# Down projection by seven block products: operand sums from the up stage, residual summed in DRAM

## The chip, the core and the metric

One core of a Trainium2 chip runs the whole kernel. Its engines work side by side, each on its own queue in order: TensorE (PE, with PEld for its weight loads), VectorE (DVE), ScalarE (ACT), GpSimd (POOL) and SyncE (SP). DMA transfers are issued here from SP's and POOL's queues. The metric is the device time of one execution in microseconds (us). Three executions of the kernel before took 2852.30, 2852.07 and 2847.18 us, median 2852.07.

## The reference

One layer of a hybrid decoder on 512 prompt tokens and 8 x 4 sample tokens, all in float32, model width 2048, feed-forward width 5504. Attention (two groups of heads) comes first; the part that matters here is the feed-forward block with a causal convolution of width 3 over the tokens, and the gate behind it:

```
def conv_ffn(xn, prefix, w_up, conv_w, conv_b, w_down):
    L = xn.shape[1]
    a, u = jnp.split(xn @ w_up, 2, axis=-1)
    a_all = jnp.concatenate([prefix.astype(a.dtype), a], axis=1)
    c = a_all[:, 0:L] * conv_w[0] + a_all[:, 1:L + 1] * conv_w[1] + a_all[:, 2:L + 2] * conv_w[2] + conv_b
    h = jax.nn.gelu(c) * u
    return h @ w_down, a_all[:, -(CONV_W - 1):]
...
        f, conv_new = conv_ffn(rmsnorm(h, ffn_norm_g[i]), conv_s[i], ffn_w_up[i], ffn_conv_w[i],
                               ffn_conv_b[i], ffn_w_down[i])
        h = h + f
        h = h + jax.nn.sigmoid(h @ ple_w_gate[i] + ple_b_gate[i]) * (p[i] @ ple_w_proj[i])
    y = rmsnorm(h, final_norm_g)
```

## The kernel before

**Layout.** Features lie on the 128 partitions, tokens are columns: 544 of them, as two halves of 272 (256 prompt and 16 sample tokens each). The width 2048 is 16 tiles of 128 rows, the feed-forward width 5504 is 43 tiles, which I call hidden tiles.

**Products.** A float32 product is made from two parts of each number, a high part (a cast, on ACT) and a low part (the difference, on DVE), and three matmuls: high by high, high by low, low by high (`product`, line 176; `multiply`, line 1146). So weights are loaded raw by SP, cast to wh by ACT (line 166, or 1138 in up) and subtracted to wl by DVE (167 or 1139), and the moving operands are split in the same way (886 and 887). One matmul is 128x128 weights by 128x272 columns.

**Up.** For each hidden tile, `up` computes both the gate half a and the linear half u of the tile for both halves of the tokens. That is a product of a 2x2 block matrix of weights by a 2x2 block matrix of operands (blocks of 8 of the 16 width tiles), and it is made by seven products in place of eight, from sums of blocks: the operand sums a11, s1, s2, a12, s3, s4, a22 lie in SBUF for the whole stage, and the weight sums are made per tile by DVE on the raw tiles (lines 1171, 1177, 1187, 1194). Each product is 8 x 3 = 24 matmuls, 168 a tile, into three PSUM banks X, Y, Z. The sums over the results, the normalisation, the convolution and the gelu follow on DVE, ACT and POOL (lines 1196 to 1217); the hidden tile uu goes to DRAM (hd, line 1218, by SP). POOL copies the last rows of the convolution into one tile cvo for all hidden tiles (lines 1205 and 1206), stored once at the end.

**Down.** The residual, 16 tiles resid, comes back from DRAM (rd, line 1254, by POOL). Then two phases of 22 and 21 hidden tiles: POOL loads each hidden tile (hr, line 1262), ACT and DVE split it into hh and hl, which stay in SBUF for the phase; for each of the 16 output tiles, 6 matmuls per hidden tile (three, for two halves of the columns) into one PSUM tile, which DVE adds to resid (line 1271). 

**Gate and end.** resid is split into h2, the gate product (16 x 96 matmuls) and the per-layer embedding follow, then the final normalisation.

**What sets the order.** A scheduler puts each engine's instructions in a fixed order when the kernel is built; on the chip each engine's queue runs in that order and waits by semaphores. Buffers come from pools with a number of turns (`bufs`): an instruction that writes the next turn waits until the readers of the old one are done. In this program a DMA of SP or POOL is issued only when the eighth one before it on the same queue has landed.

## Time and profile before

| what | value |
|---|---|
| times of three runs | 2852.30, 2852.07, 2847.18 us |
| the profiled execution's own time | 2849.02 us |
| its span | 2847.2 us |
| mean granted clock of TensorE | 0.978 |
| PE busy in the span | 2747.2 us, 96% |
| DVE, ACT, POOL busy | 1549.0, 1026.9, 381.0 us |
| up, steady part | about 1330 to 2042 us of the span |
| down | 2067.6 to 2622.2 us |
| gate | 2622.2 to 2820.2 us |

The profiled execution is 3.0 us below the median of the three. Busy times of engines overlap. A busy PE includes matmuls at the lower clock, so the granted clock stands beside it wherever a stretch is read. An instruction's mean is over all its occurrences in the run.

### The profile page before, as it was taken

To read this page: it belongs to the slowest core of one execution; us is meant where nothing else is said; L and a number is where in the kernel's file an instruction comes from. 1 tells how busy PE (TensorE), PEld (TensorE's weight loads), DVE (VectorE), ACT (ScalarE), POOL (GpSimd) and SP (SyncE) were. 2 spreads that over 40 slices of the span, in tenths; PEclk is the share of its full clock that TensorE was granted. 3 is DMA by queue.
4 is the path that set the end of the run, shared out by engine and by line. 5 is a ranking of instruction groups with operands and counts; after the bars stand their busy time and mean duration, and the time that the engine had idled before them with its cause. 6 is when DMAs were issued, how large, how long until landed. Compare 5 with 4: busy or idle time off the path is not lost.

```text
span 2847.2 us, 50928 instructions
## 1 busy us (share of the span) xinstructions
PE 2747.2 (96%) x21730; PEld 2681.2 (94%) x21730; DVE 1549.0 (54%) x2245; ACT 1026.9 (36%) x1621; POOL 381.0 (13%) x492
## 2 busy tenths in 40 slices
PE   8999999999999999899999999999959999999996
PEld 7989999999999789899999999999959999999996
DVE  5034433322256668878888888888742224223344
ACT  4034323221135455544544445445431113112331
POOL 6610101101201300111111111111130001000001
PEclk9999999999999999999999999999979999999998
DMA  6422222332524814333333333433273225223321
GB/s 228 149 72 77 93 91 84 109 106 94 196 75 175 294 51 143 116 112 112 106 129 102 114 121 101 126 110 107 77 265 94 85 86 160 87 89 102 113 91 68
DMA packets 103699, 335.36 MB, mean 118 GB/s; under 512 B 13105, under 2 KB 17857, under 8 KB 100401
## 3 DMA queue, kind: packets, MB, share of 16 engines
q1 hardware_dynamic: 86432, 271.76, 29.0%
q0 software_dynamic: 17040, 60.36, 6.4%
q8 instruction: 170, 2.79, 0.4%
q14 instruction: 57, 0.46, 0.0%
HBM read 289.87 MB, written 42.19 MB: 117 GB/s over the span
## 4 chain that ended last, share of the span: by engine, by line
PE 82%; issue 10%; DMA 3%; DVE 3%; POOL 1%; ACT 1%; SPq 0%; DVEq 0%; POOLq 0%; ACTq 0%
PE mp L176 35%; PE X L1146 18%; PE Y L1146 9%; PE mq L176 6%; PE Z L1146 4%; DMA hr<-hd 2%; PE sp L357 2%; PE sp L963 1%; PE sp L923 1%; PE sp L593 1%; POOL rows L336 1%; PE sp L944 1%; PE so L585 1%; DMA raw<-in_w_out 0%; DVE resid L1325 0%
## 5 line engine op out<-in xcount | busy, mean ns | idle before, releaser
L167 DVE TENSOR_TENSOR wl<-raw,wh 128x1024 fp32r<-128x1024 f32 (+3 forms) x271 | 307.9, 1138 | 538.1 <-ACT wh L166 514.0
L166 ACT CAST wh<-raw 128x1024 fp32r<-128x1024 f32 (+3 forms) x271 | 263.9, 976 | 846.5 <-PE mp L176 629.2
L1138 ACT CAST wh<-raw 128x1024 fp32r<-128x1024 f32 x301 | 312.3, 1051 | 369.7 <-PE X L1146 153.1
L1139 DVE TENSOR_TENSOR wl<-raw,wh 128x1024 fp32r<-128x1024 f32 x301 | 363.9, 1220 | 63.5 <-ACT wh L1138 61.5
L176 PE MATMUL mp<-xl,wh 128*128 128x272 f32 x1408 | 303.3, 294 | 0.0
L176 PE MATMUL mp<-xh,wl 128*128 128x272 f32 x1408 | 301.3, 294 | 0.0
L176 PE MATMUL mp<-xh,wh 128*128 128x272 f32 x1408 | 300.0, 293 | 0.0
L176 PEld LDWEIGHTS mp<-xh,wl 128*128 128x128 f32 x1408 | 225.8, 191 | 5.7 <-issue 5.2
L176 PEld LDWEIGHTS mp<-xl,wh 128*128 128x128 f32 x1408 | 225.8, 191 | 4.3 <-issue 3.7
L176 PEld LDWEIGHTS mp<-xh,wh 128*128 128x128 f32 x1408 | 225.0, 191 | 4.0 <-issue 2.7
L176 PE MATMUL mp<-hh,wh 128*128 128x272 f32 x946 | 198.8, 292 | 28.8 <-ACT hh L886 28.8
L176 PE MATMUL mp<-hl,wh 128*128 128x272 f32 x946 | 196.9, 290 | 0.7 <-DVE hl L887 0.7
L176 PE MATMUL mp<-hh,wl 128*128 128x272 f32 x946 | 196.8, 290 | 0.0
L176 PEld LDWEIGHTS mp<-hh,wh 128*128 128x128 f32 x946 | 149.2, 190 | 30.3 <-ACT hh L886 30.3
L176 PEld LDWEIGHTS mp<-hl,wh 128*128 128x128 f32 x946 | 150.1, 190 | 2.0 <-DVE hl L887 1.9
L1205 POOL COPY cvo<-ae 128x2 f32<-128x2 f32 x43 | 51.6, 1200 | 738.8 <-DVE ae L1202 738.8
L176 PEld LDWEIGHTS mp<-hh,wl 128*128 128x128 f32 x946 | 149.4, 190 | 0.1
L1146 PE MATMUL Y<-s,wh 128*128 128x272 f32 x688 | 133.3, 289 | 4.7 <-ACT uu L1174 4.7
L1146 PE MATMUL X<-a,wh 128*128 128x272 f32 x688 | 131.3, 288 | 0.0
L1146 PEld LDWEIGHTS Y<-s,wh 128*128 128x128 f32 x688 | 109.0, 190 | 5.0 <-ACT uu L1174 5.0
L1146 PEld LDWEIGHTS X<-a,wh 128*128 128x128 f32 x688 | 108.4, 189 | 0.2 <-DVE uu L1189 0.2
L1146 PE MATMUL Z<-a12h,wh 128*128 128x272 f32 x344 | 99.9, 291 | 0.4 <-ACT wh L1138 0.4
(463 smaller groups left out, 6932.6 us busy)
## 6 DMA issues: line engine op xcount, KB each, us to landing
raw<-in_w_up SPq DMA_DIRECT2D x172, 512.0 KB, 4.6
raw<-in_w_in SPq DMA_DIRECT2D x89, 512.0 KB, 3.5
raw<-in_w_dn SPq DMA_DIRECT2D x64, 512.0 KB, 3.6
raw<-in_w_gate SPq DMA_DIRECT2D x32, 512.0 KB, 3.7
raw<-in_w_out SPq DMA_DIRECT2D x24, 512.0 KB, 3.8
hd<-uu SPq DMA_DIRECT2D x43, 272.0 KB, 5.4
hr<-hd POOLq DMA_DIRECT2D x43, 272.0 KB, 3.4
w<-in_cmp_w POOLq DMA_DIRECT2D x8, 1024.0 KB, 7.4
```

The costliest lines, as they stand in the source:

```text
L166: nc.scalar.copy(wh[:, :m], raw[:, s:s + m])
L167: nc.vector.tensor_sub(wl[:, :m], raw[:, s:s + m], wh[:, :m].bitcast(F32))
L176: nc.tensor.matmul(pp[g][:, :GN] if isinstance(pp, list) else pp[:, g, :GN], w, x[:, g], start=first, stop=last)
L336: nc.gpsimd.indirect_dma_start(out=out, out_offset=None, in_=I[cache], in_offset=bass.IndirectOffsetOnAxis(ap=idx[:, 4 * b + pg:4 * b + pg ...
L357: nc.tensor.matmul(at[j // 16], w1[j // 16][:, j % 16], rows[:, :, j % 16], start=j == 0, stop=j == 31, skip_group_check=True)
L585: nc.tensor.matmul(sos[dv][:, b * 4:b * 4 + 4], S0[r // 2][:, r % 2, dv * 128:dv * 128 + 128], smp[:, 1, b * 4:b * 4 + 4], start=False, st ...
L593: nc.tensor.matmul(ss[r][:, :256], kdm[q4, m], vs_t[q4], start=True, stop=True, tile_position=(32 * r, 0))
L923: nc.tensor.matmul(s[:, :n0], qv, K[:, 0, :n0], start=True, stop=True)
L1138: nc.scalar.copy(wh, raw)
L1139: nc.vector.tensor_sub(wl, raw, wh.bitcast(F32))
L1146: nc.tensor.matmul(ps[:, :GN], w[wi][:, k], a[k][xi], start=start and k == 0 and i == 0, stop=stop and k == n - 1 and i == 2, skip_group_c ...
L1205: nc.gpsimd.tensor_copy(cvo[:, c, 0:2], ae[:, 512:514])
```

## The change

Down is made by seven block products, as up is already. The 2x2 blocks are: of the hidden tiles, k and k + 21 (21 pairs, and tile 42 alone); of the output, tiles 2n and 2n + 1; of the tokens, the two halves. In detail:

- `UP_ORDER` runs up over the hidden tiles in pairs (0, 21, 1, 22, ...), tile 42 last. After each pair, `pair_operands` makes the operand sums with four DVE adds of 128x272, and SP stores seven operands of 136 KB to DRAM (names dd_...) in place of two hidden tiles of 272 KB. A sign is moved so that uu is a plain product.
- The rows for the convolution are loaded and stored per tile by POOL (cpre 128x16, cvo 128x18) in place of one tile for all.
- Down has three phases of 7 pairs; the last has tile 42 as well, in four of the seven products. `load_set` loads an operand of a phase by POOL in two chunks (544 KB, and 408 or 544 KB, three buffers sg), and ACT and DVE split it into d...h and d...l, one buffer each. Sets of the next phase are loaded while the last two blocks of the present one run (`refill`).
- `down(n, ph)` loads four weight tiles of 128x896 (128x1024 where tile 42 is in), makes seven products of 21 (24) matmuls in banks X, Y, Z, four weight sums on DVE, four copies from PSUM on ACT and three PSUM adds on DVE. Two values of n run interleaved product by product; "a pair of blocks" below means these two.
- The result e of each output tile is added to the residual in DRAM by an accumulating DMA of 272 KB from POOL. resid is loaded from DRAM after the last phase only, before the gate.

The new parts of down, and the sums in up:

```diff
+    def pair_operands(k, t1, t2):
+
+        ph, j = divmod(k, PK)
+        s1, s2, s4 = [stemp(fp, 4) for _ in range(3)]
+        n11, a21, n12, a22 = t1[:, 0], t1[:, 1], t2[:, 0], t2[:, 1]
+        nc.vector.tensor_add(s1, a21, a22)
+        nc.vector.tensor_add(a21, a21, n11)
+        nc.vector.tensor_add(s2, s1, n11)
+        nc.vector.tensor_add(s4, s2, n12)
+        for name, src in zip(DSETS, (n11, s1, s2, n12, a21, s4, a22)):
+            nc.sync.dma_start(ddram[name, ph][:, j], src)
...
+    def load_set(name, ph):
+        n = set_size(name, ph)
+        pl = dl if name in ("s4", "a22") else dr
+        hl = [pl.tile([128, PK + 1, GN], F32R, tag=name + c, bufs=1, name=f"d{name}{c}") for c in "hl"]
+        for j in range(0, n, 4):
+            m = min(4, n - j)
+            t = dp.tile([128, 4, GN], F32, tag="sg", bufs=3, name="sg")
+            nc.gpsimd.dma_start(t[:, :m], ddram[name, ph][:, j:j + m])
+            f = lambda a: a.rearrange("p k n -> p (k n)")
+            split_scaled([f(a[:, j:j + m]) for a in hl], f(t[:, :m]), -1.0 if name == "s2" else None)
+        D_[name] = [[a[:, j] for a in hl] for j in range(n)]
+
+    def down(n, ph, after):
+        r11, r12, r22, r21 = [next_raw(I["w_d%s%d" % ("ab"[u], ph)][2 * n + j], PK + (u == 0 and ph == PHASES - 1))
+                              for j, u in ((0, 0), (1, 0), (1, 1), (0, 1))]
+        ka, kb = set_size("a11", ph), PK
+        e = [dp.tile([128, G, GN], F32, tag=f"e{j}", bufs=3, name=f"e{j}") for j in range(2)]
+        p1, c21, u2, y5 = e[0][:, 0], e[0][:, 1], e[1][:, 0], e[1][:, 1]
+        X, Y, Z = bank("X"), bank("Y"), bank("Z")
+        multiply(X, parts(r11, ka, True), D_["a11"], True, False)
+        nc.scalar.copy(p1, X[:, :GN])
+        after("a11")
+        yield
+        nc.vector.tensor_sub(r11[:, :ka], r12[:, :ka], r11[:, :ka])
+        multiply(Y, parts(r11, ka), D_["s1"], True, False)
...
+        multiply(X, parts(r21, kb), D_["a22"], False, True)
+        nc.scalar.copy(c21, X[:, :GN])
+        for j in range(2):
+            nc.gpsimd.dma_start(rdram[2 * n + j], e[j], accum_op=ALU.add)
+        after("a22")
...
+    for name in DSETS:
+        load_set(name, 0)
+    for ph in range(PHASES):
+        def refill(name, ph=ph):
+            load_set(name, ph + 1)
+        for n in range(0, HK, 2):
+            last = n == HK - 2 and ph < PHASES - 1
+            together([down(n, ph, nothing), down(n + 1, ph, refill if last else nothing)])
```

POOL's queue at the seam between up and down, before: the last residual loads, the copies of the last hidden tile, and the first hidden-tile loads.

```order
L1254 DMA resid_22005<-rd_10686 128x544
L1254 DMA resid_22005<-rd_10687 128x544
L1205 COPY cvo<-ae 128x2
L1206 COPY cvo<-ae 128x16
L1254 DMA resid_22008<-rd_10688 128x544
L1254 DMA resid_22008<-rd_10689 128x544
L1262 DMA hr<-hd_11646 128x544
L1262 DMA hr<-hd_11647 128x544
```

After, at the same place: the copies and conv stores of the last two tiles, and behind them the loads of the operand sets (dd_a and dd_s are the operands a.. and s.. in DRAM).

```order
L1218 DMA out_conv<-cvo 128x18
L1216 COPY cvo<-ae 128x2
L1217 COPY cvo<-ae 128x16
L1218 DMA out_conv<-cvo 128x18
L1294 DMA sg<-dd_a_11646 128x1088
L1294 DMA sg<-dd_a_11646 128x816
L1294 DMA sg<-dd_s_11649 128x1088
L1294 DMA sg<-dd_s_11649 128x816
```

The residual loads are gone from this place, and each hidden tile's conv rows are now stored from POOL, ahead of the first operand load.

ACT's order in down, before: casts of hidden tiles (hh) between the weight casts (wh).

```order
L166 CAST wh<-raw 128x768
L886 CAST hh<-hr 128x544 x4
L166 CAST wh<-raw 128x1024
L886 CAST hh<-hr 128x544 x3
L166 CAST wh<-raw 128x1024
L886 CAST hh<-hr 128x544 x3
L166 CAST wh<-raw 128x640
```

After, where the last pair of blocks of the first phase begins: copies from PSUM into e, weight casts, and the casts of the next phase's operand sets (da11h, ds1h) from sg.

```order
L1335 COPY e_23273<-X 128x272
L889 CAST wh<-raw 128x896
L1335 COPY e_23312<-X 128x272
L889 CAST wh<-raw 128x896
L1307 COPY e_23675<-X 128x272
L889 CAST wh<-raw 128x896
L1307 COPY e_23714<-X 128x272
L889 CAST da11h<-sg 128x1088
L889 CAST da11h<-sg 128x816
L889 CAST wh<-raw 128x896
L1312 COPY e_23676<-Y 128x272
L1074 ACTIVATE wh<-raw 128x896
```

The casts of an operand set now stand in ACT's queue behind the copies of the product that used the set for the last time, and ahead of weight casts of following products.

DVE's order in the tail of a hidden tile in up, before:

```order
L1194 TENSOR_TENSOR raw<-raw 128x1024
L1216 TENSOR_TENSOR gl<-gl,R_10669 128x544
L1139 TENSOR_TENSOR wl<-raw,wh 128x1024
L1217 SCALAR_TENSOR_TENSOR uu<-uu,gl 128x544
L1139 TENSOR_TENSOR wl<-raw,wh 128x1024
L1184 TENSOR_TENSOR tt<-tt,Z 128x272
L1139 TENSOR_TENSOR wl<-raw,wh 128x1024
L1189 TENSOR_TENSOR uu<-uu,X 128x272
```

After, at the end of the last pair of hidden tiles:

```order
L1228 TENSOR_TENSOR gl<-gl,R_10589 128x544
L1192 TENSOR_TENSOR raw<-raw 128x1024
L890 TENSOR_TENSOR wl<-raw,wh 128x1024
L1229 TENSOR_TENSOR uu<-uu,gl 128x544
L890 TENSOR_TENSOR wl<-raw,wh 128x1024
L1236 TENSOR_TENSOR st<-uu 128x272
L1193 TENSOR_TENSOR tt<-tt,Z 128x272
L1237 TENSOR_TENSOR uu<-uu 128x272
L1238 TENSOR_TENSOR st<-st,uu 128x272
L890 TENSOR_TENSOR wl<-raw,wh 128x1024
```

The four adds of `pair_operands` (lines 1236 to 1239) stand between weight lows (wl) of the following tile, within four weight lows behind the product with gl.

## Rows read from the trace of the kernel before

**Rows 1.** The page's first lines: the span, and for each engine its busy time in us, its share of the span and its instructions.

```profile
span 2847.2 us, 50928 instructions
...
PE 2747.2 (96%) x21730; PEld 2681.2 (94%) x21730; DVE 1549.0 (54%) x2245; ACT 1026.9 (36%) x1621; POOL 381.0 (13%) x492
```

**Rows 2.** The page's chain of work that ended last: shares of the span by engine, then by line.

```profile
PE 82%; issue 10%; DMA 3%; DVE 3%; POOL 1%; ACT 1%; SPq 0%; DVEq 0%; POOLq 0%; ACTq 0%
PE mp L176 35%; PE X L1146 18%; PE Y L1146 9%; PE mq L176 6%; PE Z L1146 4%; DMA hr<-hd 2%; PE sp L357 2%; PE sp L963 1%; PE sp L923 1%; PE sp L593 1%; POOL rows L336 1%; PE sp L944 1%; PE so L585 1%; DMA raw<-in_w_out 0%; DVE resid L1325 0%
```

**Rows 3.** Busy time in four stretches: the steady part of up, all of down, a steady piece of down, and the gate. Columns: the stretch, its length, then the busy us and the instructions of PE, PEld, DVE, ACT and POOL, the granted clock as a share, the DMA share, GB/s.

```profile
1330.00:2042.00 712.00, 712.00 (x5678) 712.00 (x5677) 595.68 (x677) 342.11 (x475) 101.91 (x136) 1.00 0.35 112
2067.60:2622.20 554.60, 525.11 (x4128) 522.28 (x4128) 162.99 (x178) 122.83 (x146) 32.57 (x62) 0.97 0.39 123
2136.00:2346.00 210.00, 210.00 (x1675) 210.00 (x1674) 51.28 (x51) 37.07 (x38) 0.00 (x0) 1.00 0.30 90
2622.20:2820.20 198.00, 195.96 (x1548) 195.52 (x1548) 81.85 (x110) 74.12 (x100) 7.05 (x14) 0.99 0.24 79
```

**Rows 4.** The same view for the length of one feed-forward tile inside up.

```profile
1330.00:1351.07 21.07, 21.07 (x170) 21.07 (x169) 17.66 (x21) 10.09 (x14) 2.99 (x4) 1.00 0.35 114
```

**Rows 5.** The chain followed in time from up into down. Columns: start us, us, what.

```profile
2064.51 3.03 PE X L1146 x24
...
2068.04 0.69 DVE ae L1202
...
2070.74 11.86 DMA resid<-rd
...
2083.16 9.83 DMA hr<-hd
```

**Rows 6.** TensorE's instructions in order of time at the start of down. Columns: start us, us (two matmuls a row, their ends overlap), what; in brackets the idle time before and what ended it.

```profile
2093.76 0.82 PE L176 MATMUL mp<-hh,wh 128*128 128x272 f32 x2 [26.23 <-ACT hh L886]
...
2095.60 0.65 PE L176 MATMUL mp<-hh,wh 128*128 128x272 f32 x2
2096.05 0.66 PE L176 MATMUL mp<-hl,wh 128*128 128x272 f32 x2
```

**Rows 7.** The view of rows 3 in steps of 4 us, at the seam between up and down and at the start of the gate.

```profile
2088.00:2092.00 4.00, 0.00 (x0) 0.00 (x0) 0.00 (x0) 0.00 (x0) 0.00 (x0) 0.50 1.03 413
2100.00:2104.00 4.00, 4.00 (x18) 3.57 (x17) 1.81 (x3) 1.24 (x3) 1.61 (x3) 0.57 0.50 151
2104.00:2108.00 4.00, 3.14 (x21) 2.65 (x21) 2.53 (x4) 2.72 (x4) 1.61 (x3) 1.00 0.50 146
...
2624.00:2628.00 4.00, 3.42 (x20) 3.20 (x19) 4.00 (x7) 4.00 (x9) 0.00 (x0) 0.71 0.35 131
2628.00:2632.00 4.00, 4.00 (x30) 4.00 (x30) 4.00 (x8) 3.77 (x7) 0.00 (x0) 0.86 0.01 4
```

**Rows 8.** DMA issues between 2060 and 2130. Columns: what, queue, count, KB of each, median us from issue to landing.

```profile
hr<-hd POOLq DMA_DIRECT2D x23, 272.0 KB, 3.4
raw<-in_w_dn SPq DMA_DIRECT2D x9, 512.0 KB, 13.9
resid<-rd POOLq DMA_DIRECT2D x16, 272.0 KB, 10.1
...
hd<-uu SPq DMA_DIRECT2D x1, 272.0 KB, 18.9
```

**Rows 9.** POOL's first copy of a tile's conv rows (duration ns min, median, max; first and last start us; forms), then POOL's issues of the hidden-tile loads of line 1262 and the time from issue to landing of those loads.

```profile
L1205 POOL COPY cvo<-ae x43: 394/1219/1222, 1194.4 to 2079.1; 128x2 f32<-128x2 f32 x43
...
L1262 POOL DMA_DIRECT2D hr<-hd x43: 537/539/553, 2083.2 to 2384.7; - x43
...
DMA to landing us min/median/max: 2.9/3.4/9.9
```

**Rows 10.** DMA issues of the whole run, from the page: KB of each and median us to landing.

```profile
raw<-in_w_up SPq DMA_DIRECT2D x172, 512.0 KB, 4.6
...
hd<-uu SPq DMA_DIRECT2D x43, 272.0 KB, 5.4
```

**Rows 11.** Groups of instructions by line: count, busy us, mean ns of one, then the idle time before them and what ended it.

```profile
L1139 DVE TENSOR_TENSOR wl<-raw,wh 128x1024 fp32r<-128x1024 f32 x301 | 363.9, 1220 | 63.5 <-ACT wh L1138 61.5 <-DMA raw<-in_w_up 2.1
L1138 ACT CAST wh<-raw 128x1024 fp32r<-128x1024 f32 x301 | 312.3, 1051 | 369.7 <-PE X L1146 153.1 <-DVE raw L1171 99.9 <-issue 66.5
...
L887 DVE TENSOR_TENSOR hl<-hr,hh 128x544 fp32r<-128x544 f32 x43 | 30.7, 724 | 47.0 <-ACT hh L886 46.7
...
L886 ACT CAST hh<-hr 128x544 fp32r<-128x544 f32 x43 | 27.6, 646 | 54.4 <-DMA hr<-hd 53.6 <-PE mp L176 0.2
...
L1184 DVE TENSOR_TENSOR tt<-tt,Z 128x272 f32<-128x272 f32 x43 | 18.8, 437 | 23.6 <-PE Z L1146 23.5
...
L1196 ACT COPY tt<-X 128x272 f32<-128x272 f32 x43 | 16.7, 387 | 58.5 <-PE X L1146 58.5
```

**Rows 12.** TensorE's instructions at the start of the gate, columns as in rows 6.

```profile
2623.62 0.52 PE L176 MATMUL mq<-h2h,wh 128*128 128x272 f32 x2 [1.43 <-ACT h2h L886]
...
2624.97 0.52 PE L176 MATMUL mq<-h2l,wh 128*128 128x272 f32 x2 [0.58 <-DVE h2l L887]
```

**Rows 13.** The gathers of selected cache rows on POOL's queue (count, median us to landing) in the stretch 900 to 1140, and the busy time of the engines in it, columns as in rows 3.

```profile
KV<-in_cache_slc,idx POOLq DMA_INDIRECT x24, 4.0
...
900.00:1140.00 240.00, 229.39 (x1924) 201.51 (x1922) 166.62 (x446) 119.16 (x318) 24.18 (x25) 0.96 0.46 162
```

More of the change, by code (lines that the diff above doesn't have):

```diff
@@ L39 @@
 S0B = 2
-PHASES = [22, 21]
+NPAIR = 21
+PHASES = 3
+PK = NPAIR // PHASES
+UP_ORDER = [k + i * NPAIR for k in range(NPAIR) for i in range(2)] + [NFF - 1]
 HK = KD // 2
@@ L1050, in trunk @@
     op_s.close()
+    r2, r2_s = pool("r2", "right")
+    R2 = r2.tile([128, G, GN], F32, name="R2")
     x2, x2_s = pool("x2", "right")
@@ L1173, in up @@
         y5 = uu[:, 1]
-        nc.scalar.copy(y5, Y[:, :GN])
+        nc.scalar.activation(y5, Y[:, :GN], AF.Copy, scale=-1.0)
         late(2)
@@ L1225, in late, with together @@
             nlate[0] += 1
-    both = [up(c, late) for c in range(2)]
-    while both:
-        both = [u for u in both if next(u, both) is None]
-    for c in range(2, NFF):
-        for _ in up(c, late):
-            pass
-    nc.sync.dma_start(O["conv"], cvo)
+    def together(gens):
+        while gens:
+            gens = [g for g in gens if next(g, gens) is None]
+    hids = []
+    for i, c in enumerate(UP_ORDER):
+        hids.append(fp.tile([128, G, GN], F32, tag="uu", bufs=4, name="uu"))
+        if i == 1:
+            together([up(UP_ORDER[j], late, hids[j]) for j in range(2)])
+        elif i:
+            together([up(c, late, hids[i])])
+        if i == NFF - 1:
+            last_operands(hids[i])
+        elif i % 2:
+            pair_operands(i // 2, hids[i - 1], hids[i])
@@ L1244, in trunk, with nothing @@
+    def nothing(name):
+        pass
+    for name in DSETS:
[6 more added lines that the diff above has]
+            together([down(n, ph, nothing), down(n + 1, ph, refill if last else nothing)])
+    dp_s.close()
+    wf_s.close()
+    dl_s.close()
+    dr_s.close()
+    st_s.close()
+    if stop == "ffn":
+        return
     mp, mp_s = psum_pool("mp")
```

133 lines of the change are left out of this document (69 added, 64 removed).

## The prediction

> **What bounds the kernel now.** I start with the page's busy line and the chain of waits: TensorE is busy for 2747.2 of 2847.2 us, and 82% of the chain is its matmuls, 41% of it on the product line 176 and 31% on the three banks of line 1146 [rows 1, 2]. VectorE is at 54%, but that is a mean over stages, so the windows come next. In the up stage (1330 to 2042) PE is busy for all 712.00 us at full clock, 5678 matmuls, so 0.1254 us each; in a steady piece of down (2136 to 2346) it is 1675 in 210.00, again 0.1254 [rows 3]. So in both stages a matmul that disappears gives back 0.1254 us, as long as nothing else takes over. VectorE is the nearest: 17.66 of the 21.07 us of one feed-forward tile in up [rows 4], but only 51.28 of 210 in down.
>
> The second place to look is the seam between the stages. From 2067.60 to 2622.20 there are 4128 matmuls, which at 0.1254 need 517.7 of the 554.6 us: 36.9 are lost. The chain says where: after the last up matmul (2064.51 + 3.03) the tail of that tile, then a resid load of 11.86 us and an hr load of 9.83 [rows 5]. PE sits 26.23 us idle and then runs a matmul in about 0.227 us (2095.60 to 2096.05 for two) [rows 6], at the lower clock level (granted 0.50 in the idle stretch, 0.57 until 2104, then 1.00, that is 1.2 against 2.4 GHz) [rows 7]. The idle stretch is a burst of transfers, at 413 GB/s in that row, in which everything lands late: resid loads 10.1 us, weights 13.9, the last hidden tile's store 18.9 [rows 8].
>
> **The sum**, against the profiled run's 2849.0 us.
>
> 1. Matmuls. Down has now 6 per hidden tile and output tile: 43 x 16 x 6 = 4128. After, each block of two output tiles takes seven products of 3 matmuls per pair of hidden tiles, and four products contain the odd tile: 8 x (21 x 7 + 4) x 3 = 3624. That is 504 fewer, of the same 128x272 form: 504 x 0.1254 = **-63.2**. Up keeps its 168 a tile.
>
> 2. The seam. Removed: the 16 resid loads at its head. Added: POOL must make two copies into cvo (the first takes 1.22 us [rows 9]) and start the conv store before it issues the first sg load, all in order. From the last up matmul, ae is ready at +1.2 us and the copies end near +3.5 to +4.5; the first sg load of 544 KB is issued at about +5.7 and lands at about +9.5 (a 512 KB weight tile takes 4.6 [rows 10]). ACT's cast and VectorE's subtraction of 1088 columns scale from 1.05 and 1.22 us for 1024 [rows 11] to 1.12 and 1.30, so PE restarts at +11 to +13. It is at the lower clock by then, as in [rows 6, 7]: the first 42 matmuls take 9.5 us, to about +23. The last tile's stores go out first, and the second set is behind them: it is loaded at about +15, split at +21. From then VectorE feeds the first pair of blocks: 12 chunk halves, 6 x (1.30 + 0.97) = 13.6; 11 weight lows of 896 columns at 1.07 = 11.8; three sums, 3.2; six PSUM adds at 0.44, 2.6; together 31 us from +20, to +51. PE ends that pair near +55, and at full rate its 294 matmuls need 36.9. So 18 to 19 lost in place of 36.9: **-18** (lost 10 to 30, so -27 to -7).
>
> 3. Two turnovers, at which the next phase's operand sets are split while the last pair of blocks runs. A normal pair costs VectorE 2 x (7 x 1.07 + 4 x 1.07 + 3 x 0.44) = 26.2 of PE's 36.9 us. The refill adds 7 x (1.30 + 0.97) = 15.9: 42.1, over by 5.2. The weight casts run two products ahead (two buffers beyond the one in use, 2 x 2.63 us), which about absorbs that, and the next pair is lighter by 10.7. I take +2 each, **+4** (0 to 12 for both): a pause of 1.43 and 0.58 us at the gate cost a stretch at granted clock 0.71 and 0.86 as well [rows 7, 12], so a small gap does not stay small.
>
> 4. The eleven joins between pairs of blocks, where copies on ACT wait in order behind one another: **+2** (0 to 8).
>
> 5. The start of the gate. Before, 2622.20 to 2820.20 holds 1536 matmuls of 0.1254, 192.6, so 5.4 lost, with the idle of [rows 12]. After, resid is read back from DRAM. All but the last four tiles are ready early, and PE has 148 gate matmuls (18.6 us) before it needs the twelfth. The path of the last tiles is a PSUM copy 0.4, POOL's issue 0.54, the accumulating transfer L, another 0.54, a load of 3.4, and 0.65 + 0.72 to split [rows 9, 10, 11]: 6.2 + L, hidden for L up to 12. First wait about 1.4 as before: **-2** (-4 to +8).
>
> 6. Up. Per pair VectorE gets four adds of 128x272 at 0.44, +0.88 us a tile: 18.5 of 21.07 [rows 4, 11]. SP gets seven stores of 136 KB in place of two of 272 KB, and they stand ahead of later weight loads. Eight raw buffers are two tiles of lead, 42 us, and a store lands in 5.4 [rows 10]. POOL gets two small transfers a tile, with 2.99 of 21.07 busy. Covered by PE: **0**. If the cover goes, a late operand add delays the loads behind its stores: 0 to +1.5 us a pair, 0 to +32, which I price as a rival.
>
> Sum: -63.2 - 18 + 4 + 2 - 2 + 0 = -77, so 2772 for the profiled run. The median of the runs shown, 2852.07, is 3.0 above 2849.0, hence about **2773**. From the ends of the terms that matter: -63.2 - 27 - 4 = -94 and -63.2 - 7 + 12 + 8 + 8 = -42, so 2758 to 2810.
>
> **Unpriced: the accumulating transfer.** No row shows one. Each adds 272 KB to DRAM; the nearest rows are a plain load of the same size, 3.4 (2.9 to 9.9 [rows 9]), and a store in a full burst, 18.9 [rows 8]. I take L = 6, nearer to the plain load, since a pair moves 3.6 MB of weights and 1.1 MB of results in 36.9 us, some 130 GB/s, a third of the burst. The buffer e exists three times, and each pair of blocks takes two, so the first copy into the second one's buffer waits for a transfer of the pair before: that copy comes 5.3 us after the pair's start, and the casts behind it on ACT are two products ahead, so L up to about 13 is free, and beyond it each us costs one at each of 11 joins.
> The Trainium skill, "Collectives: The Full Stack", section "The bandwidth ceiling: the fold count and why AG ≠ RS ≠ AR", says that a reduce in the transfer engines needs two source reads, so it sends twice the read traffic of a copy. No run here shows it yet. As an estimate by that page, four transfers of 272 KB would occupy 5.6 us in place of 2.8 at about 400 GB/s, still under the 13 that are free, so the sum stays.
>
> **Rivals.**
> (a) Turnovers and joins take back more. The chunks of a refill pass through three sg buffers. If a load under load lands in 10 us, as resid did in the burst, the ring turns three chunks in about 12 us, so 14 chunks take 56 against 36.9: 14 to 19 lost per turnover, about +30 in all, **2803** (2790 to 2830). For it: the 10.1 of [rows 8]. Against: 23 hr loads in the same window landed in 3.4.
> The skill's "SBUF — State Buffer", section "Who interferes with whom", says that a two-input VectorE operation holds off a GpSimd operation that reads SBUF; it also says that a POOL-issued DMA starves beside certain VectorE modes. The trace agrees on the copy (cvo 1.22 us in the median, in up beside a busy VectorE, 0.39 at the least [rows 9]). For the DMA it does not: the gathers on POOL landed in 4.0 us while VectorE was busy for 166.62 of 240 [rows 13], so this gives the rival no more than its 0.17.
> (b) Slower than before: the accumulating transfers land late, and ACT, waiting in order for e, holds the weight casts. It decides from L = 20 on (77 / 11 + 13); at L = 25 it costs 11 x 12 = 132, about **2904**. For it: 18.9 in the burst. Against: 3.4 at the load that down has.
> (c) Up becomes bound by VectorE or by the store queue, 1.5 us a pair, +32: **2805**. For it: 18.5 of 21.07, with the four adds in one cluster. Against: PE had no idle time at all in 712 us.
>
> **How the numbers follow.** Forecast 0.70, (a) 0.17, (c) 0.06, (b) 0.07. The first and the lower part of (a) and (c) give 2758 to 2808 as the range of eight in ten. About 0.2% (5.7 us) is what a measurement here can tell from no change. Forecast, (a) and (c) are all faster, except a tail of some 0.02 in which several come together; (b) has L between 18 and 20 for a further 0.01. So faster 0.91, same 0.03, slower 0.06.
>
> **What would show it.** 504 matmuls fewer on the page's PE row (21226 for 21730) at the same 0.125 us in the windows of both stages (step 1); the pause after the last up matmul 11 to 13 us instead of 26, and the first pair done at +55 (2); VectorE near 42 us in each refill with PE's clock at 1.00 (3); landing time of the accumulating transfers under 13 (4, rival b); no PE idle in up with VectorE near 18.5 of 21.07 (6). The forecast is wrong if steady down runs at more than 0.127 us a matmul, which I can read from any window without a turnover.

## The result and the profile after

The changed kernel takes 2781.27 us (median of four, 2776.22 to 2783.17) against 2849.62 for the kernel before (median of four): a ratio of 0.9758, with a 95% interval of 0.9739 to 0.9777. The forecast of 2773 was 8 us too low and the range held. The profiled execution took 2782.99 us, 66.0 less in its span than the one before (2781.2 against 2847.2).

The page's first lines and its chain, which answer to [rows 1, 2]:

```profile
span 2781.2 us, 51019 instructions
...
PE 2688.2 (97%) x21226; PEld 2623.7 (94%) x21226; DVE 1780.0 (64%) x2537; ACT 1136.5 (41%) x1788; POOL 472.4 (17%) x624
...
PE 83%; issue 8%; DMA 3%; DVE 3%; POOL 2%; ACT 1%; SPq 0%; DVEq 0%; POOLq 0%; ACTq 0%
PE mp L179 30%; PE X L1155 24%; PE Y L1155 12%; PE Z L1155 6%; PE mq L179 3%; PE sp L360 2%; PE sp L596 1%; PE sp L966 1%; DMA KV<-in_cache_slc,idx 1%; POOL rows L339 1%; DMA sg<-dd_a 1%; DMA sg<-dd_s 1%; POOL KV L339 1%; PE so L588 1%; PE sp L926 0%
```

TensorE has 504 matmuls less and is still busy for 97% of the span. Down's matmuls now stand under the banks X, Y and Z together with those of up; the loads of hidden tiles are gone from the chain, and the operand loads (sg) have 2% of it. VectorE went from 1549.0 to 1780.0 us, in a shorter span.

The windows that answer to [rows 3]: steady up, then down cut at its seam and its two turnovers, columns as there.

```profile
1330.00:2042.00 712.00, 712.00 (x5678) 712.00 (x5677) 619.08 (x744) 341.69 (x475) 137.67 (x202) 1.00 0.38 123
2068.99:2130.00 61.01, 41.86 (x300) 40.92 (x300) 48.06 (x53) 31.69 (x42) 17.14 (x23) 0.83 0.67 224
2130.00:2240.00 110.00, 110.00 (x875) 110.00 (x874) 85.57 (x93) 55.44 (x77) 14.93 (x21) 1.00 0.61 166
2240.00:2260.00 20.00, 17.93 (x140) 17.42 (x139) 18.87 (x19) 10.85 (x18) 3.96 (x6) 1.00 0.74 211
2260.00:2390.00 130.00, 130.00 (x1032) 129.89 (x1031) 98.44 (x108) 63.45 (x85) 16.94 (x23) 1.00 0.61 171
2390.00:2420.00 30.00, 27.13 (x193) 26.68 (x192) 23.78 (x23) 14.77 (x21) 2.84 (x4) 0.89 0.48 127
2420.00:2558.25 138.25, 138.25 (x1097) 138.04 (x1096) 95.32 (x102) 59.17 (x81) 19.35 (x27) 1.00 0.55 144
```

Up runs without a pause, with the same 5678 matmuls in 712 us; VectorE does 619.08 us in place of 595.68. Down ends at 2558.27, 489.3 us after the last up matmul (2068.99), where it was 554.7. At 0.1254 us a matmul, 300 of them are worth 37.6 of the first 61.01 us: 23.4 lost. ("Lost" is always the length of a stretch less 0.1254 us for each of its matmuls.) The turnovers lose 2.4 (20.00 less 140 x 0.1254) and 5.8 (30.00 less 193 x 0.1254). In the three steady rows nothing beyond 1.6 us is lost in all. The same cut of the kernel before:

```profile
2067.54:2110.00 42.46, 13.48 (x64) 11.75 (x65) 15.46 (x20) 12.53 (x19) 14.32 (x28) 0.64 0.87 314
2110.00:2622.20 512.20, 511.63 (x4066) 510.52 (x4065) 147.53 (x158) 110.33 (x128) 18.31 (x34) 1.00 0.35 107
```

There 42.46 us held 64 matmuls, 8.0 us worth, so the seam lost 34.4, and the rest of down 2.3.

TensorE's pauses above 0.5 us in the changed kernel, columns as in [rows 6]; but for one of 0.50 behind the first, these are all of them between 2068.99 and the gate's start:

```profile
2085.14 0.82 PE L1155 MATMUL X<-da11h,wh 128*128 128x272 f32 x2 [16.15 <-ACT da11h L889]
...
2096.88 0.39 PE L1155 MATMUL Y<-ds1h,wl 128*128 128x272 f32 x1 [0.71 <-DVE wl L890]
...
2101.58 0.40 PE L1155 MATMUL X<-ds2h,wh 128*128 128x272 f32 x1 [1.79 <-ACT wh L889]
...
2250.18 0.39 PE L1155 MATMUL Y<-ds1h,wh 128*128 128x272 f32 x1 [1.46 <-ACT wh L889]
...
2251.30 0.39 PE L1155 MATMUL X<-ds2h,wh 128*128 128x272 f32 x1 [0.60 <-ACT wh L889]
...
2402.43 0.40 PE L1155 MATMUL Y<-ds1h,wh 128*128 128x272 f32 x1 [1.43 <-ACT wh L889]
...
2404.39 0.60 PE L1155 MATMUL X<-ds2h,wh 128*128 128x272 f32 x1 [1.44 <-ACT wh L889]
...
2559.56 0.53 PE L179 MATMUL mp<-h2h,wh 128*128 128x272 f32 x2 [1.30 <-ACT e L1335]
```

Two stand out. The first is the restart, 16.15 us after the last up matmul (26.23 before, [rows 6]). The four in the turnovers come in the first blocks of the new phase, on the products with s1 and s2, and a weight cast on ACT ends each.

By stages, from the two profiles:

| step | forecast, us | measured, us | from |
|---|---|---|---|
| 1 matmuls | -63.2 | -63.2 | 504 fewer, at 0.1254 |
| 2 seam | -18 | -11.0 | 34.4 lost before, 23.4 after |
| 3 turnovers | +4 | +8.2 | 2.4 and 5.8 lost |
| 4 joins | +2 | -0.7 | the rest of down: 2.3 lost before, 1.6 after |
| 5 gate and end | -2 | -2.1 | from the last down matmul to the end, 225.0 before, 222.9 after |
| 6 up | 0 | -5.9 | first to last up matmul, 914.8 before, 908.9 after |
| before up | 0 | +7.4 | first up matmul at 1152.69 before, 1160.09 after |
| sum | -77 | -67 | the spans: -66.0 |

The last row but one is not put down to the change: in the profiles below, kernels that differ from the changed one behind that point alone have their first up matmul anywhere from 1150.97 to 1160.13 (on two chips; a third is some 30 us later), and the same kernel again has it at 1154.28. The prediction's sign for step 2, the first pair of blocks done at +55, did not come either: its 294 matmuls end 60.6 us after the last up matmul, and 57.3 in the second profile.

### The profile page after: what moved, and what is told of

Read it like the earlier page. It is cut to its first block, busy times and chain, and to the rows that moved or that the text cites. A ratio compares the mean times of both kernels' runs of the same rounds, so it can differ in the third digit from the quotient of the medians.

```text
span 2781.2 us, 51019 instructions
## 1 busy us (share of the span) xinstructions
PE 2688.2 (97%) x21226; PEld 2623.7 (94%) x21226; DVE 1780.0 (64%) x2537; ACT 1136.5 (41%) x1788; POOL 472.4 (17%) x624
## 4 chain that ended last, share of the span: by engine, by line
PE 83%; issue 8%; DMA 3%; DVE 3%; POOL 2%; ACT 1%; SPq 0%; DVEq 0%; POOLq 0%; ACTq 0%
PE mp L179 30%; PE X L1155 24%; PE Y L1155 12%; PE Z L1155 6%; PE mq L179 3%; PE sp L360 2%; PE sp L596 1%; PE sp L966 1%; DMA KV<-in_cache_slc,idx 1%; POOL rows L339 1%; DMA sg<-dd_a 1%; DMA sg<-dd_s 1%; POOL KV L339 1%; PE so L588 1%; PE sp L926 0%
## 5 line engine op out<-in xcount | busy, mean ns | idle before, releaser
L889 ACT CAST wh<-raw 128x1024 fp32r<-128x1024 f32 (+1 forms) x397 | 405.3, 1031 | 491.3 <-PE X L1155 229.7
L890 DVE TENSOR_TENSOR wl<-raw,wh 128x1024 fp32r<-128x1024 f32 (+1 forms) x397 | 471.4, 1196 | 84.6 <-ACT wh L889 84.4
L169 ACT CAST wh<-raw 128x1024 fp32r<-128x1024 f32 (+1 forms) x175 | 171.9, 985 | 482.2 <-PE mp L179 398.4
L170 DVE TENSOR_TENSOR wl<-raw,wh 128x1024 fp32r<-128x1024 f32 (+1 forms) x175 | 201.3, 1153 | 258.8 <-ACT wh L169 235.1
L1074 ACT ACTIVATE wh<-raw 128x896 fp32r<-128x896 f32 (+1 forms) x72 | 69.4, 965 | 104.8 <-PE X L1155 46.3
L1075 DVE SCALAR_TENSOR_TENSOR wl<-raw,wh 128x896 fp32r<-128x896 f32 (+1 forms) x72 | 79.4, 1104 | 34.3 <-ACT wh L1074 34.3
L1155 PE MATMUL X<-a11h,wh 128*128 128x272 f32 x344 | 100.1, 291 | 0.0
L1155 PE MATMUL X<-a11l,wh 128*128 128x272 f32 x344 | 99.7, 290 | 0.0
L1155 PE MATMUL X<-s2h,wh 128*128 128x272 f32 x344 | 99.6, 289 | 0.0
L1155 PE MATMUL X<-s2h,wl 128*128 128x272 f32 x344 | 98.9, 288 | 0.4 <-DVE wl L890 0.4
```

Of the source, the lines that this page charges most:

```text
L169: nc.scalar.copy(wh[:, :m], raw[:, s:s + m])
L170: nc.vector.tensor_sub(wl[:, :m], raw[:, s:s + m], wh[:, :m].bitcast(F32))
L889: nc.scalar.copy(hi, src)
L890: nc.vector.tensor_sub(lo, src, hi.bitcast(F32))
L1074: nc.scalar.activation(hl[0], src, AF.Copy, scale=scale)
L1075: nc.vector.scalar_tensor_tensor(hl[1], src, scale, hl[0].bitcast(F32), op0=ALU.mult, op1=ALU.subtract)
```

## The experiments

The kernels ran on three chips: the first four below that change the computation or the conv rows (`a12_twice`, `no_refill`, `plain_store`, `conv_off_pool`) on one, `after_again` and the three `tail_first`, `tail_conv`, `tail_conv_pool` on a second, the last four on a third. On the first everything ahead of up took some 30 us more (first up matmul at 1183 to 1186), so totals compare only by the ratio to the kernel before on the same chip. The changed kernel itself was not run on that chip, and its two ratios elsewhere, 0.9758 and 0.9726, differ by 9 us, so what I compare is the stage: from the last up matmul to the last down matmul. "Stage" below is always that time; it is 489.3 us in the first profile of the changed kernel and 487.1 in the second, so differences of some 2 us mean nothing. The totals in the expectations are meant against the 2781 of the first measurement.

**One product twice.**

```diff
-        multiply(Z, parts(r21, kb, True), D_["a12"], True, True)
+        w21 = parts(r21, kb, True)
+        multiply(Z, w21, D_["a12"], True, True)
+        multiply(Z, w21, D_["a12"], True, True)
```

> The product with a12 is made twice in every block of down (the second overwrites the first): 8 x 3 x 21 = 504 more matmuls, nothing more on the other engines. If TensorE bounds down, +504 x 0.1254 = +63, less up to 8 us that the turnovers between phases no longer lose, since VectorE gets more time per pair of blocks: 2836 to 2846 against 2781 for the changed kernel, a ratio of 0.995 to 0.999 to the kernel before. Rival: the gain of the change came from elsewhere and down is paced by VectorE or by transfers: then the extra matmuls are partly hidden and the time is below 2820.

2863.17 us, ratio 0.994 (0.9921 to 0.9959). The row of the stage:

```profile
2094.55:2640.43 545.88, 525.49 (x4129) 523.85 (x4128) 371.29 (x393) 235.32 (x319) 75.18 (x104) 0.98 0.55 151
```

545.9 us, 56.6 to 58.8 more than the changed kernel's 489.3 and 487.1, for 504 more matmuls worth 63.2. The missing 4 to 7 us are in the turnovers: their pauses above 0.4 us add up to 2.3 us here and to 4.9 in the changed kernel, and with the matmuls at the lower clock behind them the turnovers lose 3.3 us here against 8.7 and 9.8 there. The ratio is just below the 0.995 to 0.999 expected, and the rival is refuted: TensorE bounds down, and a matmul there costs what step 1 says.

**No operands for the later phases.**

```diff
         def refill(name, ph=ph):
-            load_set(name, ph + 1)
+            D_[name] = (D_[name] * 2)[:set_size(name, ph + 1)]
```

> The operands of the second and third phase are left out: no loads and no splits at the turnovers, the products run on the first phase's operands. If the two turnovers cost the 8 us that the windows show (2.4 and 5.8), TensorE has no pause there and the time is 2771 to 2776 against 2781. Rival: the pauses there only take up time that would be lost later (the accumulating transfers or the weight loads hold the joins): within 3 us of 2781.

Ratio 0.970 (0.9678 to 0.9721), and the stage:

```profile
2094.87:2572.32 477.45, 459.88 (x3624) 458.90 (x3624) 341.75 (x365) 208.35 (x290) 59.87 (x76) 0.98 0.56 142
```

477.5 us, 10 to 12 less, with no pause above 0.4 us after the first blocks. Not all of that is the turnovers, since the seam differs from profile to profile. The first 62 us of the stage, in the changed kernel twice and in this one:

```profile
2068.99:2130.99 62.00, 42.85 (x308) 41.91 (x308) 49.05 (x54) 32.45 (x43) 17.14 (x23) 0.83 0.68 223
2063.15:2125.15 62.00, 44.87 (x333) 44.28 (x334) 51.01 (x58) 32.73 (x43) 18.00 (x24) 0.86 0.73 234
2094.87:2156.87 62.00, 44.43 (x332) 43.67 (x333) 51.37 (x58) 32.78 (x44) 16.39 (x21) 0.86 0.69 206
```

They lose 23.4, 20.2 and 20.4 us, and the rest of the stage 11.4, 12.4 and 2.6. So down's losses are the seam and the turnovers and little else, and the turnovers cost 9 to 10 us in all, somewhat more than the 8.2 of the windows.

**Plain stores in place of accumulating ones.**

```diff
-            nc.gpsimd.dma_start(rdram[2 * n + j], e[j], accum_op=ALU.add)
+            nc.gpsimd.dma_start(rdram[2 * n + j], e[j])
```

> The accumulating transfers become plain stores of the same size (the sum with the residual and over the phases is left out). My theory: the accumulation is hidden, time 2777 to 2785, the same pauses of TensorE in down, and the landing time falls from 4.5 to about 3. Rival: the accumulating transfers hold buffers or bandwidth and pace the joins or the seam: at least 8 us faster, below 2773.

Ratio 0.9718 (0.97 to 0.9736), the stage:

```profile
2093.78:2578.70 484.92, 462.63 (x3624) 460.32 (x3624) 369.14 (x393) 233.71 (x318) 59.66 (x104) 0.98 0.51 170
```

484.9 us, 2.2 to 4.4 less, about as much as two profiles differ, and the pauses in the turnovers stay (4.4 us in all). By the stage the rival, 8 us or more, is refuted: the accumulation does not pace down; that it costs 2 or 3 us is not excluded. Whether plain stores land in 3 us, as expected, this profile does not tell. Its own rows in the changed kernel are POOL's issue of line 1337, the time from issue to landing, and what ACT's first copy into e (line 1307) waited for it (us, times):

```profile
L1337 POOL DMA_DIRECT2D rd<-e x48: 847/860/1203, 2122.7 to 2560.2; - x48
...
DMA to landing us min/median/max: 3.8/4.5/9.2
...
  DMA rd<-e: 5.6, 2
```

L is 4.5 us in the median and 9.2 at most, where I had taken 6 and allowed 13. Two copies waited, 5.6 us together, one in each turnover (1.84 us at 2247.5 and 3.77 at 2399.2), where the transfers are at 0.98 of their share and more; in the second profile one did, for 1.6 us.

**The unchanged kernel again, and the order at the seam.** In the changed kernel these are VectorE's first instructions after the last up matmul (2068.99), and POOL's (start us, us, what; in brackets the idle time before):

```profile
2069.60 2.09 DVE L1075 SCALAR_TENSOR_TENSOR wl<-raw,wh 128x896 fp32r<-128x896 f32 x2 [3.15 <-ACT wh L1074]
2071.61 2.09 DVE L1310 TENSOR_TENSOR raw<-raw 128x896 f32<-128x896 f32 x2
2073.62 0.68 DVE L1212 TENSOR_TENSOR ae<-tt,R 128x512 f32<-128x512 f32 x1
...
2074.36 3.09 POOL L1216 COPY cvo<-ae 128x2 f32<-128x2 f32 x1 [22.38 <-DVE ae L1212]
2077.39 1.79 POOL L1217 COPY cvo<-ae 128x16 f32<-128x16 f32 x1
...
2080.24 1.07 POOL L1294 DMA_DIRECT2D sg<-dd_a  x2 [0.23 <-issue]
2086.70 1.59 POOL L1294 DMA_DIRECT2D sg<-dd_s  x3 [5.39 <-DMA dd_s<-st]
```

The normalisation of the last hidden tile (ae) starts 4.6 us after the matmul: two weight lows and two weight sums of down stand ahead of it. POOL's two copies then take 3.09 and 1.79 us, and behind them the first operand load is issued at +11.25. The second operand's load waits for the stores of the same hidden tile (I take it that its buffer lies where that tile was): +17.7.

Several kernels change this. `conv_off_pool` moves the copies of the conv rows to ACT and their store to SP:

```diff
-        nc.gpsimd.tensor_copy(cvo[:, 0:2], ae[:, 512:514])
+        nc.scalar.copy(cvo[:, 0:2], ae[:, 512:514])
...
-        nc.gpsimd.dma_start(O["conv"][:, c], cvo)
+        nc.sync.dma_start(O["conv"][:, c], cvo)
```

> The two small copies of each tile's conv rows go from POOL to ACT and their store from POOL to SP; all else as in the changed kernel. Theory: the first operand load of down waited only for its turn behind these copies (3.09 and 1.79 us for the last tile), so it is now issued before the last up matmul instead of 11.3 us after it, TensorE restarts 5 to 9 us after that matmul instead of 16.15, and the time is 4 to 9 us lower, 2772 to 2777. Rival: VectorE's work in the seam (about 31 us for the first pair of blocks) sets its end: TensorE restarts earlier but the first pair ends as late, and the time stays within 2 us of 2781.

Ratio 0.9735 (0.9716 to 0.9753). The first operand load was issued 5.8 us before the last up matmul, but TensorE restarted only 12.61 us after it: the cast of the operand stood on ACT behind the gelu of the last hidden tile, which waited for VectorE. The stage is 485.5, 1.6 to 3.8 less, so of the restart at +5 to +9 and the gain of 4 to 9 us neither came. The first pair of blocks ends at +58.5, between the 57.3 and 60.6 of the changed kernel, which is the rival's answer.

`after_again` is the changed kernel as it is; `tail_first` orders ACT and VectorE by dependencies that only set the order of issue: on VectorE everything of down's first pair of blocks stands behind the tail of the last hidden tile, on ACT behind that tile's last copy from PSUM.

```diff
+    behind = ExitStack()
+    for k in ("act", "dve"):
+        behind.enter_context(tc.issue_after(edge[k].ins))
     for name in DSETS:
         load_set(name, 0)
...
             together([down(n, ph, nothing), down(n + 1, ph, refill if last else nothing)])
+            behind.close()
```

> The changed kernel unchanged, for the stages on the same chip as the three others. From the last up matmul to the last down matmul 485 to 490 us, TensorE restarts 15 to 16 us after the last up matmul, pauses of 2 to 3 us in each turnover; ratio to the kernel before 0.973 to 0.978.

> Only the order at the seam is changed: on VectorE and ACT the work for the first blocks of down stands behind the tail of the last hidden tile, not in it. Theory: the seam is late because seven weight operations (7.4 us) stand in that tail on VectorE, so ae, the two copies of the conv rows, the first operand load and the stores that free the buffer of the second operand all come 4 to 6 us late. Then the last hidden tile is done about 7 us after the last up matmul instead of 13.3, the first operand load is issued at about +5 instead of +11.3, TensorE restarts at +9 to +11, and the time is 5 to 7 us below the changed kernel's. Rival: the sum of VectorE's work in the first pair of blocks (31 us) sets its end whatever the order: TensorE restarts earlier, but the stage is within 2 us.

`after_again`: 2772.43 us, ratio 0.9726 (0.9706 to 0.9746). `tail_first`: 2769.55, ratio 0.9728 (0.9702 to 0.9755). Its POOL and ACT at the seam (last up matmul at 2061.59):

```profile
2062.87 0.18 POOL L1217 COPY cvo<-ae 128x2 f32<-128x2 f32 x1 [18.29 <-DVE ae L1213]
2062.99 0.20 POOL L1218 COPY cvo<-ae 128x16 f32<-128x16 f32 x1
...
2064.25 1.07 POOL L1295 DMA_DIRECT2D sg<-dd_a  x2 [0.23 <-DMA raw<-in_w_db]
...
2072.07 0.94 ACT L889 CAST wh<-raw 128x896 fp32r<-128x896 f32 x1 [5.09 <-DVE raw L1311]
2072.92 1.87 ACT L889 CAST da11h<-sg 128x1088 fp32r<-128x1088 f32 x2
```

The copies that took 3.09 and 1.79 us take 0.18 and 0.20, the first load is issued at +2.7. But TensorE restarts at +12.48 (14.67 in `after_again`), since the operand's cast stands behind a weight cast that waits 5.09 us for a weight sum on VectorE, and pauses again for 3.36 us for the low part. The stage is 486.7 against 487.1, the time that the rival gave; whether for the rival's reason, VectorE's sum, is asked below.

`tail_conv` joins both edits:

> The order of tail_first, and the copies of the conv rows on ACT with their store on SP. Theory: the first operand load no longer waits for anything in the tail but the buffer of tt, TensorE restarts at +6 to +8, then waits for the second operand, whose buffer is that of the last hidden tile; 6 to 9 us below the changed kernel. Rival: the second operand decides alone: same as tail_first within 1 us.

Restart at +12.67 in place of +6 to +8, stage 486.6, ratio 0.9734 (0.9713 to 0.9756): as `tail_first`.

`tail_conv_pool` lets POOL make low parts at the turnovers:

```diff
+            if ph and j and name != "s2":
+                nc.scalar.copy(pair_[0], f(t[:, :m]))
+                nc.gpsimd.tensor_sub(pair_[1], f(t[:, :m]), pair_[0].bitcast(F32))
```

> tail_conv, and at the two turnovers POOL makes the low part of the second chunk of six of the seven operands: about 6 us per turnover leave VectorE, 42 to 36 of the 36.9 us that TensorE needs for that pair of blocks. Theory: VectorE's overload makes the pauses there: below 1 us in each turnover, no stretch at the lower clock, 4 to 9 us below tail_conv. Rival: POOL's subtractions beside a busy VectorE take so long (as the copy of 3.09 us in the seam) that the operands come later: the pauses grow and the time is above tail_conv's.

Ratio 0.9744 (0.9724 to 0.9764), stage 488.4; the pauses of the turnovers are 7.0 us in all against 5.8 in `tail_conv`. One of the groups of POOL's subtractions (ns min, median, max), and the pair of blocks with the first refill and the pair behind it, in `tail_conv` and then here:

```profile
L1300 POOL TENSOR_TENSOR da11l<-sg,da11h x2: 2282/2462/2643, 2200.2 to 2356.2; 128x816 fp32r<-128x816 f32 x1, 128x1088 fp32r<-128x1088 f32 x1
...
2200.68:2278.90 78.22, 75.17 (x590) 74.29 (x589) 65.64 (x71) 43.35 (x58) 14.43 (x22) 1.00 0.74 212
2191.48:2273.05 81.57, 77.00 (x590) 75.89 (x589) 69.78 (x65) 43.26 (x58) 27.31 (x28) 0.98 0.69 204
```

VectorE takes 1.00 and 1.29 us for these two sizes, POOL 1.9 to 3.6. The theory failed, for a reason that neither it nor the rival had: VectorE has six operations fewer and is busy for longer, 69.78 us in place of 65.64 (at the second turnover 72.13 in place of 67.61). Beside each of POOL's twelve subtractions stands a VectorE operation that takes 2.1 to 3.4 us, where its like take 1.09 or 1.22. So the run did not take load off VectorE, and it does not say whether VectorE's overload makes the pauses. That they grew, as the rival has it, is within what two profiles differ by (1.2 us, and 1.7 in the stage).

**The first operand ahead of the other weights, and the buffers.** `tail_a11` is `tail_first` with the split of a11 ahead of the weight work of the second and later products; `sg4_e2` is the changed kernel with other numbers of buffers; `tail_a11_sg4` has both.

```diff
-            t = dp.tile([128, 4, GN], F32, tag="sg", bufs=3, name="sg")
+            t = dp.tile([128, 4, GN], F32, tag="sg", bufs=4, name="sg")
...
-        e = [dp.tile([128, G, GN], F32, tag=f"e{j}", bufs=3, name=f"e{j}") for j in range(2)]
+        e = [dp.tile([128, G, GN], F32, tag=f"e{j}", bufs=2, name=f"e{j}") for j in range(2)]
```

> tail_first, and the split of the first operand (a11) stands ahead of the weight work of the second and later products on ACT and VectorE. In tail_first its first load had been issued at +2.7 us but its cast stood behind a weight cast that waited 5.1 us for VectorE, and its low part behind six weight operations. If such in-order places set the seam: TensorE restarts at +7.5 to +9 without the pause of 3.4 us behind it, and the stage from the last up matmul to the last down matmul is 479 to 483 us against 487. Rival: the ring of three buffers through which all 14 chunks of the operands come, each released by VectorE, sets the end of the first pair of blocks: 485 to 488 as before, the pause only moves to a later product.

> The changed kernel with four buffers for the operand chunks in place of three; to make room, two buffers for the results e in place of three. If the ring of three holds up the operands, the first pair of blocks ends 3 to 6 us earlier and the pauses in the turnovers shrink from 2 to 3 us to about 1: the stage 480 to 484 us against 487. If VectorE's work sets it, the stage is within 2 us of 487. For the joins my step 4 says that an accumulating transfer may take about 13 us with three buffers; with two it may take about 8, and it lands in 4.5, so ACT's waits for e stay under 0.5 us each.

> Both edits. If the in-order places and the ring each hold the seam for a part, the gains add up: 475 to 480 us for the stage. If one of them is what counts, it is as fast as that one alone; if VectorE's work alone counts, 485 to 488.

`tail_a11`: ratio 0.9735 (0.9715 to 0.9754). TensorE's first two pauses, and four windows of 4 us, the first from 12 us after the last up matmul (2059.65) on, the others from 20, and the first 62 us as above:

```profile
2067.29 0.82 PE L1157 MATMUL X<-da11h,wh 128*128 128x272 f32 x2 [7.64 <-ACT da11h L891]
2070.30 0.60 PE L1157 MATMUL X<-da11l,wh 128*128 128x272 f32 x1 [2.18 <-DVE da11l L892]
```

```profile
2071.66:2075.66 4.00, 4.00 (x19) 4.00 (x19) 2.54 (x3) 1.94 (x2) 0.34 (x1) 0.50 0.94 323
...
2079.66:2083.66 4.00, 2.12 (x16) 1.90 (x15) 4.00 (x5) 2.03 (x3) 1.07 (x2) 0.94 0.54 170
2083.66:2087.66 4.00, 4.00 (x23) 4.00 (x23) 4.00 (x5) 2.04 (x3) 0.73 (x2) 0.63 0.65 217
2087.66:2091.66 4.00, 4.00 (x34) 4.00 (x34) 3.24 (x4) 4.00 (x6) 0.88 (x2) 1.00 0.71 234
...
2059.65:2121.65 62.00, 48.84 (x345) 48.08 (x346) 53.51 (x59) 34.68 (x46) 13.53 (x24) 0.86 0.75 234
```

It restarts at +7.64, half the pause of `after_again`. Then it runs at the lower clock (0.50, 19 matmuls in 4 us), pauses again for 1.88 us while VectorE is busy for all of 4.00 us, and falls to a clock of 0.63. The stage is 483.1, 4.0 less than in `after_again`, but of the 7.0 us won at the restart only 1.5 are left where the seam ends (18.7 us lost in the first 62 against 20.2): by the starts of its matmuls, the first pair has 3.4 us more of pauses behind the restart, and 40 matmuls at the lower clock in place of 20, which cost 2.1. The other 2.4 us of the stage are in the turnovers, which this edit does not touch. In the timed runs there is nothing that can be told from no change (0.9735 against 0.9726, on another chip).

`sg4_e2`: ratio 0.9731 (0.9711 to 0.975), stage 488.8, and the turnovers pause as before (2.1 and 2.8 us). With a fourth chunk buffer, and one buffer for e less, nothing is won. With two buffers for e, ACT's first copies waited for an accumulating transfer only so often (us, times):

```profile
  DMA rd<-e: 6.7, 4
```

Four times in place of two, 6.7 us in all, more than the 0.5 us each that I had expected, but at the joins inside a phase TensorE has no pause above 0.4 us. `tail_a11_sg4` restarts at +7.66 and has a stage of 488.5, ratio 0.9749 (0.9727 to 0.977). It was to be at least as fast as the better of the two, and nothing is left of the gain: its first 62 us lose 22.5, with longer pauses up to +31.7. Why the two edits together do this was not looked into.

**The up part alone.** In the profile of the kernel before, TensorE's largest pause in up is this one, in the third tile (the first two run interleaved):

```profile
1212.98 0.82 PE L1146 MATMUL Y<-s,wh 128*128 128x272 f32 x2 [4.73 <-ACT uu L1174]
```

ACT's copy into uu waited there, 2.46 us for the store of the first tile (hd<-uu), with two buffers for uu. `before_uu4` is the kernel before with the conv rows per tile, as in the change, and in the room that frees:

```diff
-        uu = fp.tile([128, G, GN], F32, tag="uu", bufs=2, name="uu")
+        uu = fp.tile([128, G, GN], F32, tag="uu", bufs=4, name="uu")
```

> The kernel before with two parts of the change alone: the conv rows loaded and stored per tile, and in the room that this frees four buffers for the hidden tile instead of two. Theory: the up stage of the changed kernel is 6 us shorter (908.9 against 914.8) since the second tile's copy into uu no longer waits for the store of an earlier tile, a pause of 4.73 us on TensorE: here up takes 908 to 910 and the time is 4 to 7 us below the kernel before, a ratio of 0.998. Rival: the pairing and its stores did it: up stays at 914 to 915.

2843.39 us against 2848.31, ratio 0.9978 (0.9964 to 0.9992). Its up stage in one row (first to last up matmul):

```profile
1149.72:2057.83 908.11, 908.11 (x7225) 907.88 (x7225) 758.60 (x879) 439.68 (x621) 170.21 (x250) 1.00 0.35 110
```

908.1 us without a pause, where the kernel before took 914.8. So 5 to 7 us of the change's gain come from up, and from neither the pairing nor the block products (the interval of the ratio alone would allow 2 to 10; the kernel before was profiled once). The two edits were not tried apart; it is the row of the pause that names the copy into uu.

## Why the prediction was right, and where it was not

- **Step 1, matmuls**, held to the size. That the same 504 put back cost 56.6 to 58.8, with the turnovers paying the rest, shows that TensorE bounds down in the changed kernel.
- **Step 2, the seam, was mis-sized**: 11.0 gained in place of 18 (14 in the second profile), and the forecast of 18 to 19 lost measured 23.4 and 20.2. The term that failed is the restart at +11 to +13, which came at +16.15 and +14.67. I had ae ready at +1.2 and the first load issued at +5.7; they came at +5.3 and +11.25, for I put the weight operations of the first blocks between the pieces of the tail and not ahead of ae, and took the copies on POOL from the median of up (1.22) where they took 3.09 and 1.79. That order alone is not the answer either: with it repaired the restart came 2.2 us earlier and the seam lost as much as before, and with the first operand ahead as well it came 7.0 earlier and the seam lost 1.5 less. What binds behind the restart is what feeds the first blocks, and not VectorE's sum of 31 us as I had it, in the changed kernel: VectorE is busy for only 7.9 of the 16 us from +12 to +28 of the second profile (2075.15 to 2091.15), and the chain of the first goes from the tail through a store of the last hidden tile (2.89 us), a load of the second operand (3.93) and one of the fourth (4.99) into ACT's queue, where a weight cast stands behind the cast of that load and ends the last pause, at +32.6. In `tail_a11` VectorE is busy for 23.2 of the 24 us from +16 to +40. Which of loads, casts and subtractions would be the limit with all the orders put right was not separated.
- **Step 3, turnovers, was half of what they cost**: 8.2 in the profile's windows and 9 to 10 when taken away. The rows show the overload that I had reckoned:

```profile
2166.20:2203.10 36.90, 36.90 (x295) 36.90 (x294) 26.02 (x29) 15.50 (x22) 3.24 (x5) 1.00 0.52 132
2203.10:2240.00 36.90, 36.90 (x296) 36.90 (x295) 33.77 (x37) 24.92 (x33) 8.38 (x14) 1.00 0.73 230
2240.00:2254.00 14.00, 11.93 (x92) 11.42 (x91) 13.62 (x14) 7.37 (x13) 3.96 (x6) 1.00 0.98 275
```

VectorE has 26.02 of 36.90 us in a normal pair of blocks (forecast 26.2). In the pair with the refill it does 33.77, and the rest is still there when the next phase begins: 13.62 of 14.00 us, and there TensorE waits. I set the two products of lead against the overshoot and took the lighter next pair as cover, but that pair begins with weight sums of its own on the same queue. That VectorE makes the pauses is not shown, though. What stands in ACT's queue just before the first of them is this:

```profile
2247.53 0.39 ACT L1307 COPY e<-X 128x272 f32<-128x272 f32 x1 [1.84 <-DMA rd<-e]
2248.42 0.87 ACT L889 CAST da22h<-sg 128x816 fp32r<-128x816 f32 x1 [0.50 <-DMA sg<-dd_a]
```

The weight cast that TensorE waits for (at 2250.18) starts behind these two at 2249.20, though its weight sum on VectorE was done at 2246.5; in the second turnover the copy at 2399.15 waits 3.77 us for an accumulating transfer, and the weight cast behind it, too, had its sum 3.5 us before. From 2226 to 2250 the transfers are at 1.03 of their share, and the chain goes through a load of the last operand that takes 7.2 us to land (7.0 in the second turnover). So the refill makes the pauses, as taking it away shows, by in-order waits for transfers on ACT in the last step; how much of it is VectorE's late release of the chunk buffers, how much the transfers themselves, no run separates: plain stores, a fourth buffer and POOL's help each left the pauses. In the second turnover the pauses of 1.43 and 1.44 us are only half of the 5.8 lost: the granted clock of that window is 0.89, so matmuls behind them ran at the lower level, as step 3 had said of small gaps.
- **Step 4 and rival (b)**: L came out at 4.5, under the 6 assumed and far from the 20 at which the change would have been slower. The mechanism was there, ACT waiting in order for e, but twice only, and at the turnovers; plain stores in their place changed 2 to 4 us.
- **Step 6, up, was left at 0 and gave 5.9**: VectorE at 18.3 of 21.07 us a tile (619.08 of 712) was hidden, as forecast, and rival (c) did not come. I overlooked the four buffers for the hidden tile, an edit of one number, though the pause that they end is in the trace of before.
- **Step 5** held. The last line of the sum has a slip: 2772 for the profiled run and the 3.0 us of the median above it make 2775 and not 2773. The sum of the steps was close by luck in part: a term too hopeful by 7 us and one too low by 4 met a gain of 6 that I had not seen. The 6 us by which the first measurement is above 2775 are, in its profile, the 7.4 ahead of up; in the second measurement the same kernel took 2772.43 against 2848.62, 76 less for a forecast of 77.

No version tried that computes the same beats the changed kernel by more than its measurement can tell.

## What to carry to other kernels

Count the saved matmuls at the rate of the steady stage, and then look at what feeds them wherever that work comes in a lump: at seams and turnovers the average share of the feeding engine says nothing. At a seam, read the built order of each in-order queue for what stands ahead of the first instruction that the next stage waits for, but follow the chain past the restart before you move it; a restart 7 us earlier left 1.5 us at the end of the seam here, and 2 us earlier nothing. Two-input work that is moved from VectorE to POOL did not leave VectorE here: its own operations beside it took two to three times as long. And read the list of buffer counts in a diff as carefully as its algorithm.
